# One of the two transfers that fill a key tile goes through GpSimd's queue instead of SyncE's

## The chip, the cores and the metric

The kernel runs on one core of a Trainium2 chip. A core has five engines that run their own instruction streams in order: TensorE (PE, matmuls), VectorE (DVE), ScalarE (ACT), GpSimd (POOL) and SyncE (SP, which here only issues transfers). They meet through semaphores. The metric is the device time of one execution in microseconds, taken as the median of three runs.

## The reference

The program computes a two-layer decoder trunk over 512 tokens of width 1024, with 16 heads of 64, in float32. Layer 0 has stick-breaking attention, layer 1 a dilated attention with rotary keys and queries; a gated feed-forward of width 2816 follows each.

```python
def _stick_breaking(q, k, v):          # per block of 128 queries
    z = jnp.einsum('bhqd,bhkd->bhqk', qb, kh).astype(jnp.float32) * scale
    log_stay = jnp.where(strict, jax.nn.log_sigmoid(-z), 0.0)
    log_after = lax.cumsum(log_stay, axis=3, reverse=True) - log_stay
    w = jnp.where(strict, jnp.exp(jax.nn.log_sigmoid(z) + log_after), 0.0)
    return jnp.einsum('bhqk,bhkd->bhqd', w, vh.astype(jnp.float32)).astype(q.dtype)
...
for layer in range(DEPTH):
    hn = _rmsnorm(h, norm_mix[layer])
    if layer < N_A_LAYERS:
        q, k, v = jnp.split(hn @ w_qkv_a[layer], 3, axis=-1)
        ...
        h = h + _stick_breaking(q, k, v).reshape(b, s, d) @ w_o_a[layer]
    else:
        kv = _rmsnorm(h, norm_kv) @ w_kv
        ...                             # rotary on the keys
        q = _rope((hn @ w_q_b[j]).reshape(b, s, N_HEADS, HEAD_DIM))
        h = h + _dilated_attention(q, kv_blocks).reshape(b, s, d) @ w_o_b[j]
    h = h + _swiglu(_rmsnorm(h, norm_ffn[layer]), w_gate[layer], w_up[layer], w_down[layer])
return _rmsnorm(h, norm_final)
```

## The kernel before

Every product is made of three matmuls on values split in a high and a low half (`mm3`, line 389): high by high, high by low, low by high. The activations lie transposed in the core's memory, channels on partitions and 512 tokens along the free axis. The stages are layer 0's attention, its feed-forward, layer 1's attention and its feed-forward.

In an attention layer the heads go in eight pairs p, heads 2p and 2p+1; this text numbers heads through both layers, 0 to 15 in layer 0 and 16 to 31 in layer 1. For each pair a projection makes 128 channels, two heads of 64, in one bank of PSUM. ACT, DVE and, in layer 1, the rotary step (`rope`, line 551, whose swap of half-heads is itself four transfers) bring it to a tile that `split_base` (line 519) splits: ACT writes the high half of a tile `hl` (line 522), DVE the low half (line 523). Then transfers rearrange it. `to_moving` (line 532) makes the key tile `mov` of each head: one head's 64 partitions of `hl`, high and low, are laid twice, into partitions 0 to 63 and 64 to 127. That is two transfers of 256 KB a tile, four a pair, 64 in all. `to_stationary` (line 539) does the like for the queries (`sta`). The scores of a head are seven matmuls z<-mov,sta (`scores`, line 639); `softmax` or `stick_breaking` makes weights of them, transposes (line 710) turn these, ACT and DVE split them into `ah` and `al` (lines 716 and 717), and `av` (line 723) multiplies with the values. Tile rings hold four `mov` tiles and two `hl`.

What fills TensorE beside a head's scores and values are pieces of the next pairs' projections. `attention` (line 733) writes the order of these pieces per head, and a scheduling layer, which has its own expectation of how long each instruction and transfer takes, sets the final fixed order of each engine's instructions. Each engine then runs in that order, and an instruction whose semaphore has not come stops everything behind it on the same engine.

SP's queue issues all transfers: the weights `raw` (line 243, 400 of them, each waiting for its ring place), `mov`, `sta`, the rotary swap `rp` (line 564), inputs and output. POOL does small things: zeros in `w`, `ah` and `al` (lines 663, 714, 715); in layer 1 the product of weights with a norm's gain (line 305) and the sine half of the rotary step (line 566); in the feed-forward a product (line 977).

Of the kernel before, what the change touches and what calls it, by code (L numbers as in the profile page):

```python
# [7 lines left out]
F = mybir.dt.float32  # L8
# [320 lines left out]
def trunk(ctx, tc, xg, wflat, cst_d, cs_d, outT):  # L329
    nc = tc.nc  # L330
    pe, act, dve, pool, sp = nc.tensor, nc.scalar, nc.vector, nc.gpsimd, nc.sync
# [26 lines left out]
    def T(name, dt=F, k=1):  # L358
        shape = [128, 512] if k == 1 else [128, k, 512]
        return rings["pool"].tile(shape, dt, name=name, bufs=rings["n"][name])  # L360
# [171 lines left out]
    def to_moving(p, hl):  # L532
        for i in range(2):
            t = T("mov", FR, 2)
            for j in range(2):
                sp.dma_start(t[64 * j:64 * j + 64].bitcast(F), hl[64 * i:64 * i + 64].bitcast(F))
            MOV[2 * p + i] = t

    def to_stationary(p, hl):
# [37 lines left out]
    def mov_pieces(layer, p):  # L577

        return proj_pieces(lambda b: to_moving(p, split_base(position(layer, b, p), 1.0)))
# [180 lines left out]
    def mixer(layer, slot0, gain_next):  # L760
        vslot = lambda p: (slot0 + p) % 9
        oslot = lambda p: (slot0 + 8 + p) % 9
        with phase(f"at{layer}", B_RINGS if layer else A_RINGS):
            def whole(fs_done):
                for f in fs_done[0]:
# [5 lines left out]
            both("qk", pair, dict(zip((3, 5, 7), rstd_steps(zb))) if layer else {})  # L771
            ends = [lambda: to_stationary(0, split_base(position(layer, pair[0], 0), 0.125)),
                    lambda: to_moving(0, split_base(position(layer, pair[1], 0), 1.0))]
            v_first, v_last = v_pieces(0, vslot, zb if layer else zbank)
            if layer == 0:
# [396 lines left out]
```

## Time and profile before

| | us |
|---|---|
| median of three runs | 1205.92 (1204.87 to 1207.19) |
| the profiled execution | 1206.22 |
| its span, first to last instruction | 1204.4 |
| TensorE busy in the span | 1185.6 (98%) |
| VectorE | 1014.0 (84%) |
| ScalarE | 698.2 (58%) |
| GpSimd | 178.6 (15%) |

The mean granted clock of TensorE is 0.997 of full. The profile's page and the trace are read so: times count from the span's first instruction, L536 is line 536 of the kernel, and tiles are named out<-in without their buffer numbers. SPq is SP's queue; a row of it shows the issue of transfers and not their movement. Idle time of an engine is put down to what ended it.

### The profile page before, as it was taken

How to read it: one execution, taken by the hardware profiler on the slowest of the kernel's cores; microseconds unless marked ns; L12 is line 12 of the kernel's file. 1: busy time of each engine (PE TensorE's matmuls, PEld its weight loads, DVE VectorE, ACT ScalarE, POOL GpSimd, SP SyncE). 2: the span in 40 equal slices, each digit the busy share in tenths (PEclk: the TensorE clock that was granted, in tenths of full speed). 3: DMA queues.
4: the chain of work that ended last, by engine and by line, in shares of the span. 5: the costliest groups of instructions: out<-in, count | busy, mean ns of one | idle time of the engine just before them, and what ended most of it. 6: DMA issues, size and time to landing. Idle time of an engine off the chain costs nothing.

```text
span 1204.4 us, 21111 instructions
## 1 busy us (share of the span) xinstructions
PE 1185.6 (98%) x7501; PEld 1059.6 (88%) x7501; DVE 1014.0 (84%) x1825; ACT 698.2 (58%) x1331; POOL 178.6 (15%) x245
## 2 busy tenths in 40 slices
PE   9999999999999999999999999999999999999997
PEld 7989888878999999999788888888889999999996
DVE  6799999899987878786868899788999978787865
ACT  6667676685545444454466677767755444445443
POOL 0000000011100000014234343110111000000111
PEclk9999999999999999999999999999999999999998
DMA  7654644234243334333154556551343333333122
GB/s 265 177 145 116 158 115 125 62 105 140 88 131 90 114 89 115 95 106 88 36 149 128 151 134 175 141 149 53 97 141 117 120 99 103 98 114 89 45 61 70
DMA packets 74361, 138.31 MB, mean 115 GB/s; under 512 B 9616, under 2 KB 13712, under 8 KB 74256
## 3 DMA queue, kind: packets, MB, share of 16 engines
q1 hardware_dynamic: 74256, 136.97, 40.0%
q8 instruction: 59, 0.97, 0.3%
q14 instruction: 46, 0.38, 0.1%
HBM read 106.00 MB, written 2.10 MB: 90 GB/s over the span
## 4 chain that ended last, share of the span: by engine, by line
PE 83%; issue 6%; DVE 5%; DMA 3%; POOL 1%; SPq 1%; ACT 1%; POOLq 0%; DVEq 0%; ACTq 0%
PE pj L387 38%; PE z L387 29%; PE t L387 10%; PE av L387 3%; PE t L710 3%; DMA raw<-wflat 1%; DVE wlo L307 1%; DMA mov<-hl 1%; DMA rp<-rp 1%; DVE H L758 1%; DVE sum L280 0%; DVE w2lo L307 0%; SPq L243 0%; DMA H<-xg 0%; POOL H L1085 0%
## 5 line engine op out<-in xcount | busy, mean ns | idle before, releaser
L306 ACT ACTIVATE whi<-raw 128x512 fp32r<-128x512 f32 (+1 forms) x290 | 178.4, 620 | 132.3 <-PE pj L387 51.2
L307 DVE TENSOR_TENSOR wlo<-raw,whi 128x512 fp32r<-128x512 f32 (+1 forms) x290 | 204.9, 714 | 25.4 <-ACT whi L306 23.1
L387 PE MATMUL pj<-VO,whi 128*128 128x512 f32 x568 | 180.8, 398 | 1.1 <-DVE H L758 1.0
L387 PE MATMUL pj<-X,whi 128*128 128x512 f32 x480 | 154.7, 402 | 0.3 <-ACT X L423 0.2
L977 POOL TENSOR_TENSOR up<-up,R 128x512 f32<-128x512 f32 x40 | 62.1, 1559 | 494.3 <-DVE up L1025 445.4
L387 PEld LDWEIGHTS pj<-VO,whi 128*128 128x128 f32 x568 | 102.4, 189 | 23.5 <-DVE H L758 2.1
L387 PE MATMUL pj<-VO,wlo 128*128 128x512 f32 x284 | 112.7, 397 | 0.0
L758 DVE TENSOR_TENSOR H<-H,pj 128x512 f32<-128x512 f32 (+1 forms) x120 | 79.2, 663 | 32.1 <-PE pj L387 31.4
L387 PEld LDWEIGHTS pj<-X,whi 128*128 128x128 f32 x480 | 87.0, 189 | 19.0 <-ACT X L423 1.0
L387 PE MATMUL z<-XT,whi 128*128 128x256 f32 x560 | 99.7, 280 | 0.0
L306 ACT ACTIVATE w2hi<-raw 128x512 fp32r<-128x512 f32 (+1 forms) x102 | 62.6, 616 | 58.0 <-PE z L387 16.6
L387 PE MATMUL z<-X,whi 128*128 128x256 f32 (+1 forms) x464 | 96.0, 301 | 0.0
L387 PE MATMUL pj<-X,wlo 128*128 128x512 f32 x240 | 95.2, 397 | 0.2 <-DVE wlo L307 0.2
L387 PEld LDWEIGHTS z<-XT,whi 128*128 128x128 f32 x560 | 86.2, 189 | 0.7
L387 PE MATMUL pj<-VO,w2hi 128*128 128x512 f32 x264 | 83.2, 396 | 0.6 <-ACT VO L983 0.4
L307 DVE TENSOR_TENSOR w2lo<-raw,w2hi 128x512 fp32r<-128x512 f32 (+1 forms) x102 | 69.8, 688 | 11.4 <-ACT w2hi L306 11.1
L387 PEld LDWEIGHTS z<-X,whi 128*128 128x128 f32 x464 | 74.9, 189 | 4.7
L387 PE MATMUL z<-XT,wlo 128*128 128x256 f32 x280 | 78.5, 280 | 0.0
L387 PE MATMUL pj<-whi,X 128*128 128x256 f32 x384 | 74.9, 284 | 2.1 <-DVE rp L565 2.1
L387 PE MATMUL z<-XT,w2hi 128*128 128x256 f32 x400 | 73.6, 283 | 0.1
L305 POOL TENSOR_TENSOR raw<-raw,H 128x512 f32<-128x512 f32 x48 | 57.5, 1209 | 82.5 <-DMA raw<-wflat 55.5
L387 PE MATMUL z<-X,wlo 128*128 128x256 f32 (+1 forms) x232 | 69.8, 301 | 0.0
(204 smaller groups left out, 3042.6 us busy)
## 6 DMA issues: line engine op xcount, KB each, us to landing
raw<-wflat SPq DMA_DIRECT2D x384, 256.0 KB, 2.8
mov<-hl SPq DMA_DIRECT2D x64, 256.0 KB, 4.4
sta<-hl SPq DMA_DIRECT2D x64, 128.0 KB, 2.3
rp<-rp SPq DMA_DIRECT2D x56, 64.0 KB, 2.2
raw<-wflat SPq DMA_DIRECT2D x16, 128.0 KB, 2.2
H<-xg SPq DMA_DIRECT2D x7, 256.0 KB, 5.3
outT<-H SPq DMA_DIRECT2D x2, 512.0 KB, 3.1
CS<-cs SPq DMA_DIRECT2D x1, 512.0 KB, 3.7
```

Of the source, the lines that this page charges most:

```text
L305: nc.gpsimd.tensor_mul(v3, v3, g.unsqueeze(2).to_broadcast([128, n // m, m]))
L306: nc.scalar.activation(hi[:, :n], v, AF.Copy)
L307: nc.vector.tensor_sub(lo[:, :n], v, hi[:, :n].bitcast(F))
L387: pe.matmul(out, a, b, start=start, stop=stop, skip_group_check=True)
L710: pe.transpose(b[:, o:o + 128], pr[i][:, 128 * c:128 * c + 128], idf)
L758: dve.tensor_add(H[:, n, e], H[:, n, e], p[:, e])
L977: pool.tensor_mul(two(u), two(u), r)
```

## The change

In `to_moving` the second transfer of each key tile, the one into partitions 64 to 127, is issued from POOL's queue. SP keeps the first.

```diff
             for j in range(2):
-                sp.dma_start(t[64 * j:64 * j + 64].bitcast(F), hl[64 * i:64 * i + 64].bitcast(F))
+
+                (sp, pool)[j].dma_start(t[64 * j:64 * j + 64].bitcast(F), hl[64 * i:64 * i + 64].bitcast(F))
```

Lines behind it have a number one higher in the changed kernel. The scheduling layer answers with other orders on all engines. On TensorE, at head 18 (tile mov_7441, first of layer 1's second pair), this stood in a row before, z_7675, z_7703 and z_7719 being the head's scores, t the transposes of an earlier head's weights and pj_7654 a projection:

```order
L710 MATMUL t_7685<-cst_67,z_7511 128x128
L710 MATMUL t_7685<-cst_67,z_7483 128x128
L710 MATMUL t_7695<-cst_67,z_7553 128x128
L710 MATMUL t_7695<-cst_67,z_7511 128x128
L710 MATMUL t_7695<-cst_67,z_7483 128x128
L387 MATMUL pj_7654<-X_62,whi_7518 128x512 x2
L387 MATMUL pj_7654<-X_62,wlo_7519 128x512
L387 MATMUL pj_7654<-X_62,whi_7518 128x512 x2
L387 MATMUL pj_7654<-X_62,wlo_7519 128x512
L387 MATMUL z_7675<-mov_7441,sta_7347 128x512 x2
L387 MATMUL z_7703<-mov_7441,sta_7347 128x384 x2
L387 MATMUL z_7719<-mov_7441,sta_7347 128x256 x3
```

and this stands there now:

```order
L711 MATMUL t_7685<-cst_67,z_7511 128x128
L387 MATMUL z_7675<-mov_7441,sta_7347 128x512 x2
L711 MATMUL t_7685<-cst_67,z_7483 128x128
L711 MATMUL t_7695<-cst_67,z_7553 128x128
L711 MATMUL t_7695<-cst_67,z_7511 128x128
L711 MATMUL t_7695<-cst_67,z_7483 128x128
L387 MATMUL z_7703<-mov_7441,sta_7347 128x384 x2
L387 MATMUL pj_7654<-X_62,whi_7518 128x512 x2
L387 MATMUL pj_7654<-X_62,wlo_7519 128x512
L387 MATMUL pj_7654<-X_62,whi_7518 128x512 x2
L387 MATMUL pj_7654<-X_62,wlo_7519 128x512
L387 MATMUL z_7719<-mov_7441,sta_7347 128x256 x3
```

The first scores stand ahead of four transposes and six projection matmuls that were ahead of them.

On TensorE at head 20 (tile mov_7887, first of the third pair), the difference between the two orders has this piece, in which the scores z_8008, z_8036 and z_8085 are added:

```order
 L387 MATMUL pj_8100<-wlo_7929,X_62 128x256
 L387 MATMUL pj_8100<-whi_7928,X_62 128x256 x2
+L387 MATMUL z_8008<-mov_7887,sta_7767 128x512 x2
+L387 MATMUL z_8036<-mov_7887,sta_7767 128x384 x2
+L387 MATMUL z_8085<-mov_7887,sta_7767 128x256 x3
 L387 MATMUL pj_8100<-wlo_7929,X_62 128x256
 L387 MATMUL pj_8100<-whi_7928,X_62 128x256
```

Before, they stood 30 matmuls later, behind the rest of this projection's piece, four transposes and most of head 19's product with the values; they have been moved past all of it.

On VectorE, ahead of the same head's keys, this stood in a row before: hl_7884 is the low half that the transfers of heads 20 and 21 wait for, wlo a split weight, ACC an addition behind an earlier head, rp the rotary step:

```order
L307 TENSOR_TENSOR wlo_7983<-raw_7569,whi_7982 128x512
L565 TENSOR_TENSOR rp_7963<-pj_7893,CS_66 128x512
L567 TENSOR_TENSOR rp_7875<-rp_7875,rp_7874 128x512
L307 TENSOR_TENSOR wlo_8047<-raw_7602,whi_8046 128x512
L630 TENSOR_TENSOR ACC_65<-av_7941,tf_8005 64x512
L523 TENSOR_TENSOR hl_7884<-rp_7875,hl_7884 128x512
```

and this now:

```order
L566 TENSOR_TENSOR rp_7963<-pj_7893,CS_66 128x512
L568 TENSOR_TENSOR rp_7875<-rp_7875,rp_7874 128x512
L307 TENSOR_TENSOR wlo_7983<-raw_7569,whi_7982 128x512
L523 TENSOR_TENSOR hl_7884<-rp_7875,hl_7884 128x512
L307 TENSOR_TENSOR wlo_8047<-raw_7602,whi_8046 128x512
L631 TENSOR_TENSOR ACC_65<-av_7941,tf_8005 64x512
```

One weight split and the addition went from before hl_7884 to behind it.

Head 24 has its scores moved forward on TensorE in the same way, past part of a projection, and head 22 past two transposes; in layer 0 only head 0's first scores move, past six projection matmuls.

## Rows read from the trace of the kernel before

**Rows 1.** Windows of the attention layers: length, busy us of PE, PEld, DVE, ACT, POOL

```profile
30.00:232.00 202.00, 202.00 (x1165) 175.57 (x1164) 179.21 (x320) 135.90 (x280) 9.97 (x78) 1.00 0.50 131
586.00:834.00 248.00, 243.07 (x1379) 209.14 (x1378) 204.49 (x501) 167.25 (x377) 73.94 (x87) 1.00 0.50 131
```

**Rows 2.** TensorE's waits in layer 1's attention: total us, times, longest us

```profile
PE pj L387 <- DVE rp L565: 2.1, 1, 2.1
PE z L387 <- DMA mov<-hl: 1.5, 3, 0.7
PE av L387 <- DVE al L717: 1.3, 3, 0.7
```

**Rows 3.** Timeline around head 18's scores: start us, us, engine, line, operation, out<-in, [idle]

```profile
649.26 3.18 SPq L536 DMA_DIRECT2D mov<-hl  x4
...
651.36 0.82 PE L710 MATMUL t<-cst,z 128*128 128x128 f32 x6
...
653.84 0.88 PE L387 MATMUL z<-mov,sta 128*128 128x512 f32 x3 [0.26 <-DMA mov<-hl]
```

**Rows 4.** The key tile's own view: its transfers, from issue to landing

```profile
DMA to landing us min/median/max: 2.9/4.4/5.6
```

**Rows 5.** Chain that ended last, at head 18's keys: start us, us, what

```profile
649.81 3.90 DMA mov<-hl
```

**Rows 6.** Groups of instructions on POOL, the gain product: count, busy us, mean ns

```profile
L305 POOL TENSOR_TENSOR raw<-raw,H 128x512 f32<-128x512 f32 x48 | 57.5, 1209 | 82.5 <-DMA raw<-wflat 55.5 <-DVE s L1015 13.7 <-DVE st L688 6.8
```

**Rows 7.** Timeline around head 0's scores

```profile
32.32 3.23 SPq L536 DMA_DIRECT2D mov<-hl  x4
...
36.66 0.63 PE L387 MATMUL pj<-X,whi 128*128 128x512 f32 x2
...
38.06 0.63 PE L387 MATMUL z<-mov,sta 128*128 128x512 f32 x2
```

**Rows 8.** Timeline around head 4's scores

```profile
77.63 3.65 SPq L536 DMA_DIRECT2D mov<-hl  x4
...
82.87 0.71 PE L387 MATMUL z<-mov,sta 128*128 128x512 f32 x2
```

**Rows 9.** Timeline around head 20's keys and scores

```profile
677.14 2.49 POOL L305 TENSOR_TENSOR raw<-raw,H 128x512 f32<-128x512 f32 x2
...
677.21 1.51 DVE L567 TENSOR_TENSOR rp<-rp 128x512 f32<-128x512 f32 x1 [0.59 <-POOL rp L566]
...
678.65 1.52 DVE L307 TENSOR_TENSOR wlo<-raw,whi 128x512 fp32r<-128x512 f32 x1
...
678.76 0.63 ACT L522 ACTIVATE hl<-rp 128x512 fp32r<-128x512 f32 x1 [0.74 <-DVE rp L567]
...
680.70 1.18 DVE L523 TENSOR_TENSOR hl<-rp,hl 128x512 fp32r<-128x512 f32 x1
...
681.15 0.28 PE L387 MATMUL pj<-wlo,X 128*128 128x256 f32 x1
...
682.40 0.39 PE L387 MATMUL av<-al,VO 128*128 128x256 f32 x1 [0.72 <-DVE al L717]
...
683.33 0.68 DVE L567 TENSOR_TENSOR rp<-rp 128x512 f32<-128x512 f32 x1
...
686.52 0.70 PE L387 MATMUL z<-mov,sta 128*128 128x512 f32 x2 [0.54 <-DMA mov<-hl]
```

**Rows 10.** Timeline around the scores of heads 22 and 24

```profile
706.43 0.70 PE L387 MATMUL z<-mov,sta 128*128 128x512 f32 x2 [0.69 <-DMA mov<-hl]
...
732.81 0.36 PE L387 MATMUL pj<-whi,X 128*128 128x256 f32 x1
...
734.50 0.70 PE L387 MATMUL z<-mov,sta 128*128 128x512 f32 x2
```

**Rows 11.** Chain that ended last, at layer 1's first rotary keys

```profile
628.28 4.80 DMA rp<-rp
```

**Rows 12.** DMA issues of the page, the rotary swap: KB each, median us to landing

```profile
rp<-rp SPq DMA_DIRECT2D x56, 64.0 KB, 2.2
```

## Prediction

> **What bounds the kernel now.** I read the stages first, then who waits for whom, then the key tiles' own path. By stage [rows 1], TensorE is busy in 202.00 of the 202.00 us of layer 0's attention and in 243.07 of 248.00 us in layer 1's, so time can be won or lost only where the matmul queue stands still: about 5 us in layer 1, nothing in layer 0. The waits of layer 1 name what stops it [rows 2]: once the rotary output (2.1 us), three times the key transfers themselves (1.5 us), three times the low half of the attention weights (1.3 us). Key transfers are therefore on the path in layer 1, and just hidden in layer 0.
>
> One pair of heads costs four transfers, all on SP's queue: the row at 649.26 [rows 3] has four in 3.18 us. They land 2.9 us after issue at best, 4.4 in the middle and 5.6 at worst [rows 4]. For the tile of head 18 the second half was issued at 649.81, 0.55 after the first, and took 3.90 us to 653.71 [rows 5]; so an even tile is whole 4.45 us after its first issue. Its scores began at 653.84 after 0.26 us of idle [rows 3]: 0.13 us pass between landing and matmul.
>
> **The change part by part.** Removed: 32 of 64 issues on SP, about 1.6 us of each pair's 3.18 [rows 3]. Added: 32 transfers on POOL's queue, each pair behind a wait for the low half of `hl` by DVE. Nothing in the trace shows a transfer issued by POOL, so I bound the shift of an even tile, s, from both sides. Below: both halves land as the quickest does, 2.9 us after the wait, against 4.45, so s = -1.5. Above: POOL needs as long for one issue as for its gain product, 1.21 us [rows 6], and the transfer then takes the worst landing: 1.21 + 5.6 - 4.45 = +2.4. I take s = 1.21 - 0.55 = +0.66, rounded to +0.6: POOL starts 1.21 us late, but the half no longer stands 0.55 us behind its sister. Odd tiles gain, but nobody is waiting for them.
>
> The Trainium skill bears on the low bound. Its page "DMA: Bandwidth & Descriptors", section "Rules for kernel authors", says that spreading transfers over issuing engines brings no bandwidth, because the same 16 engines carry them; it saves issue time alone. By that rule s could not be -1.5, about 0 at best; the sum below does not use it, and no run here shows it yet.
>
> The scheduler also answers to the edit: it expects keys earlier and puts their scores ahead of other work in TensorE's fixed order. A matmul placed too early stops everything behind it. Term by term:
>
> - Head 0: the first half was issued at 32.32, so the tile is whole near 36.77 (an estimate, + 4.45), and its scores stand at 38.06 [rows 7]. They now stand six projection matmuls earlier, at 36.66. With s they can start at 36.77 + 0.6 + 0.13 = 37.50: cost 0.8 us.
> - Heads 4, 8, 12 (their place is kept): 77.63 + 4.45 + 0.6 + 0.13 = 82.81 against the score's 82.87 [rows 8]: cost 0. The cover is TensorE's earlier work; it is thin, so each 0.1 us that s is above 0.66 costs 0.1 three times.
> - Head 18: the scores move to behind the second of six transposes, that is 651.57 in the old times (651.36 plus two steps, an estimate from 0.82 us for six that overlap [rows 3]). The keys come at 653.84 at the old pace, with s at 654.44. The idle is 2.87 instead of 0.26: cost 2.6 us. The work it was moved past comes afterwards and no longer hides the transfer.
> - Head 20: all seven score matmuls move from 686.52 to just before 681.15 [rows 9]. DVE's order moves too: `hl` goes ahead of a weight split begun at 678.65 and an addition, and could start when ACT's half is done (678.76 + 0.63 = 679.4) instead of 680.70 [rows 9], 1.3 us sooner. The scores then start at 686.52 - 1.3 + 0.6 = 685.8. The work jumped over lasts 686.52 - 681.15 = 5.37 us less its two idles (0.72 and 0.54), 4.1 us, and follows the scores. TensorE reaches the old end 685.8 + 4.1 - 686.5 = 3.4 us late. This is a total, not on top of head 18's 2.6, if the keys don't slide with TensorE; it is on top if they do.
> - Head 22 jumps two transposes in front of a wait of 0.69 us [rows 10]: 0.2 + s, about 0.8.
> - Head 24 moves from 734.50 to 732.81 [rows 10], where there is no idle now: 1.7 + s = 2.3.
>
> If no lateness carries over, layer 1 costs 3.4; if all does, 2.6 + 3.4 + 0.8 + 2.3 = 9.1. The keys come out of TensorE's own projections, but through ACT, DVE, POOL and transfers with waits of their own; I take a third of the way, 5.3. Against it stands SP's relief. The rotary transfer of 4.80 us [rows 11] had queued behind four key and four weight transfers; its kind takes 2.2 in the middle [rows 12], and TensorE lost 2.1 us to that chain [rows 2]. The new order also fills that gap with other projections, but head 18's keys then arrive no sooner, which is why I credit only 1.5. Sum: 0.8 + 5.3 - 1.5 = +4.6 us. What is queued behind POOL's new waits (memsets in layer 0, gain and rotary products in layer 1) costs nothing in the sum, since no wait in [rows 2] names POOL as the one that came last; if a gain product came late by the two issues' 2.4 us, the weights would be used up at once and that would appear as a new wait.
>
> The profiled execution took 1206.22 us (span 1204.4); 1206.2 + 4.6 = 1210.8. It ran 0.3 above the median shown, so for a median I say 1210.5.
>
> **The rivals.**
>
> 1. *No change*: no lateness carries over, and the work that the scores were moved past fills all the other idle of layer 1. For it: the three kinds of waits in [rows 2] sum to only 4.9 us and can swap places; against it: layer 0 has no idle to give. Sum: 0.8 + 3.4, less 2.1 (rotary), 1.3 (attention weights) and 0.7 (head 22), is +0.1: time 1206.3.
> 2. *Faster*: two queues work side by side, halves land together, s = -1.5. Every s above becomes 2.1 smaller: head 0 costs nothing, head 18 costs 0.5, and the total at head 20 is 3.4 - 2.1 = 1.3, the only lateness if none carries over. Off that go the rotary wait (2.1), the waits for attention weights (1.3), which displaced work now fills, and head 22's 0.69 [rows 2, 10]: 1.3 - 2.1 - 1.3 - 0.7 = -2.8, time 1203.4. It decides from s below about -1.3, and only if nothing carries over. Against it: the four scores moved forward use up whatever the tile gains.
> 3. *Much slower*: POOL can't issue while DVE works. For it: the two engines slow each other in the trace; the same DVE rotary addition takes 1.51 us at 677.21, while POOL is at work from 677.14, and 0.68 at 683.33 when it is alone [rows 9]. If each issue waits out two such DVE instructions, 3 us, s is about +2.4. Heads 4, 8 and 12 then cost 1.75 each (5.2), head 0 2.6, layer 1 about 5.3 + 4 x 1.8 = 12.5 before the credit of 1.5. Sum +19, time 1225; with half of it absorbed, 1216. Against it: POOL's row there is a product that reads two operands, and an issue reads none. The Trainium skill has the mechanism on its page "SBUF — State Buffer", section "SBUF: two separate sides": GpSimd writes the descriptors of its own transfers and is locked out while DVE runs in a two-port mode. The trace agrees only in that the pair slows down together.
>
> **How the numbers follow.** Forecast 0.55, no change 0.21, faster 0.12, much slower 0.12. 0.2% of this kernel is 2.4 us, about what a measurement tells from no change. Of the forecast's own spread (1207.5 to 1215) a little falls within that, of rival 1 a little beyond: faster 0.12, same 0.23, slower 0.65. The range 1203.5 to 1219 leaves out half of the faster case and the upper half of the much slower one.
>
> **What would show it.** In the profile after: POOL has 32 transfers, SP 32 fewer; the second half of an even tile lands 4.5 to 5.5 us after DVE's `hl`; TensorE waits for keys four to six times in layer 1, 1 to 3 us each at heads 18, 20 and 24, against 1.5 us in all now; the 2.1 us wait for rotary output is gone or shorter; layer 0 grows by about 1 us at its first head and nowhere else; both feed-forward stages keep their length. I am wrong if the waits for keys sum to less than 3 us (the scheduler's guess was good), if layer 0 grows by over 3 us (POOL's issue is far dearer than 1.21 us), or if the time is lost in new waits for weights.

## The result and the profile after

The changed kernel takes 1221.72 us (median of four, 1217.85 to 1224.95) beside 1206.2 for the kernel before on the same chip: a ratio of 1.0130, 95% interval 1.0116 to 1.0144, or 15.5 us more. The prediction had the side right and the size wrong: 4.6 us more was forecast (1210.5), and 1221.7 lies above its range.

The profiled execution after took 1224.95 us (span 1223.1); it is the slowest of the four, 3.2 above their median. Windows of the two attention layers, with the columns of [rows 1] (length, busy us of PE, PEld, DVE, ACT, POOL, granted clock, DMA share, GB/s), and under them four stretches of layer 1:

```profile
30.00:235.00 205.00, 202.13 (x1160) 175.12 (x1159) 178.92 (x320) 135.51 (x279) 18.11 (x94) 1.00 0.50 129
589.00:852.00 263.00, 249.66 (x1378) 215.43 (x1377) 204.97 (x501) 168.88 (x376) 79.76 (x103) 0.97 0.48 124
658.50:661.80 3.30, 3.30 (x12) 2.91 (x11) 2.42 (x8) 1.80 (x4) 0.02 (x1) 0.50 0.84 240
692.60:695.90 3.30, 3.30 (x17) 3.28 (x15) 3.04 (x11) 0.00 (x0) 0.94 (x1) 0.50 0.98 255
743.80:750.50 6.70, 5.75 (x24) 5.56 (x25) 4.75 (x10) 1.18 (x3) 3.12 (x3) 0.50 0.61 163
801.80:805.20 3.40, 3.40 (x9) 2.62 (x9) 3.40 (x13) 2.06 (x4) 0.00 (x0) 0.50 0.66 151
```

Layer 0 grew by 3 us, layer 1 by 15, and what lies between kept its length. New is the third number from the right: in four stretches of layer 1, 17 us together, TensorE ran at half of its clock, 1.2 GHz. The profile of before has the half level only from 1196.8 us on, at the last matmuls. TensorE's waits, first layer 1's (which answers to [rows 2]), then layer 0's, where the same view of the kernel before is empty:

```profile
PE z L387 <- DMA mov<-hl: 8.3, 3, 3.3
PE pj L387 <- DVE rp L566: 2.3, 1, 2.3
PE z L387 <- issue: 1.2, 1, 1.2
PE t L711 <- DVE z L697: 1.0, 1, 1.0
PE av L387 <- DVE al L718: 0.5, 1, 0.5
```

```profile
PE z L387 <- issue: 2.5, 1, 2.5
PE pj L387 <- DVE tq L549: 0.4, 1, 0.4
```

Waits for keys in layer 1 rose from 1.5 us to 9.5 (8.3 by name, and 1.2 put down to "issue" at head 16, whose keys landed 0.1 us before its scores). The other three are at heads 18, 20 and 24. From the timeline the scores of head 16, head 18's surroundings, which answer to [rows 3], and the scores of heads 20 [rows 9] and 24; the columns are start, length, engine, line, operation, tiles and idle before:

```profile
630.22 1.05 PE L387 MATMUL z<-mov,sta 128*128 128x512 f32 x4 [1.25 <-issue]
...
653.43 1.14 SPq L537 DMA_DIRECT2D mov<-hl  x2
...
653.65 1.08 POOL L537 DMA_DIRECT2D mov<-hl  x2 [0.84 <-DVE hl L523]
...
654.82 0.38 PE L711 MATMUL t<-cst,z 128*128 128x128 f32 x2
...
657.79 0.73 PE L387 MATMUL z<-mov,sta 128*128 128x512 f32 x2 [2.58 <-DMA mov<-hl]
...
658.36 0.97 PE L711 MATMUL t<-cst,z 128*128 128x128 f32 x4
...
692.03 2.07 PE L387 MATMUL z<-mov,sta 128*128 128x512 f32 x7 [3.34 <-DMA mov<-hl]
...
744.75 1.86 PE L387 MATMUL z<-mov,sta 128*128 128x512 f32 x4 [2.33 <-DMA mov<-hl]
```

Head 18's scores stand behind the second transpose, the four others follow them, and TensorE stands for 2.58 us where it stood for 0.26. The seven scores of head 20 take 2.07 us, most of it at half clock; before, the chain that ended last has them in 1.41:

```profile
686.52 1.41 PE z L387 x7
```

The transfers themselves, with the issue's duration (min, median, max ns), the landing (min, median, max us, which answers to [rows 4]), and the median by queue:

```profile
L537 POOL DMA_DIRECT2D mov<-hl x32: 509/512/720, 31.1 to 812.9; - x32
L537 SPq DMA_DIRECT2D mov<-hl x32: 462/538/762, 32.0 to 812.6; - x32
...
DMA to landing us min/median/max: 3.0/5.2/8.0
```

```profile
mov<-hl POOLq DMA_DIRECT2D x32, 256.0 KB, 5.7
mov<-hl SPq DMA_DIRECT2D x32, 256.0 KB, 5.1
```

POOL issues as fast as SP, 0.51 us, right behind DVE's low half; yet the transfers land later on both queues than the 4.4 of before.

### The profile page after: what moved, and what is told of

Same layout as the page of the kernel before. It is cut to its first block, busy times and chain, and to the rows that moved or that the text cites. A ratio compares the mean times of both kernels' runs of the same rounds, so it can differ in the third digit from the quotient of the medians.

```text
span 1223.1 us, 21168 instructions
## 1 busy us (share of the span) xinstructions
PE 1193.3 (98%) x7501; PEld 1066.3 (87%) x7501; DVE 1015.6 (83%) x1825; ACT 699.8 (57%) x1331; POOL 192.3 (16%) x277
## 4 chain that ended last, share of the span: by engine, by line
PE 81%; DVE 6%; issue 6%; DMA 3%; ACT 1%; POOL 1%; SPq 0%; POOLq 0%; DVEq 0%; ACTq 0%
PE pj L387 36%; PE z L387 29%; PE t L387 10%; PE av L387 3%; PE t L711 2%; DVE wlo L307 1%; DMA mov<-hl 1%; DMA raw<-wflat 1%; DVE H L759 1%; DMA rp<-rp 1%; DVE sum L280 0%; DVE rp L568 0%; DVE w2lo L307 0%; DVE z L689 0%; DVE sum L281 0%
## 5 line engine op out<-in xcount | busy, mean ns | idle before, releaser
L307 DVE TENSOR_TENSOR wlo<-raw,whi 128x512 fp32r<-128x512 f32 (+1 forms) x290 | 207.9, 724 | 28.0 <-ACT whi L306 25.7
```

What stands on the lines that cost most here:

```text
L307: nc.vector.tensor_sub(lo[:, :n], v, hi[:, :n].bitcast(F))
```

## The experiments

The change does two things at once: it moves transfers, and it makes the scheduling layer write another order. The first two runs take these apart. A function pins every engine to a list of instructions; it adds no waits, only an order of issue (the last run of this section, pinned too, takes as long as the kernel before, so the pinning costs nothing that can be seen):

```diff
+def hold(nc, tc):
+    traced = {i.name: i for i in nc.cur_bb.bb.instructions}
...
+            if prev is not None:
+                tc.add_manual_dep(i, prev.name, mybir.DependencyInfo(
+                    mybir.DependencyClass.NoSync, mybir.DependencyReason.DATA), reason="hold")
+            prev = i
...
         trunk(ctx, tc, *ins, out)
+        hold(nc, tc)
```

**The queue without the order.** The changed kernel, with the list of the kernel before on every engine:

> The second halves go out from POOL as in the change, but every engine keeps the order of issue of the kernel before (POOL's 32 transfers stand where SP issued their first halves). Theory A, the new order of the matmuls is what costs: an even tile is whole 4.3 to 4.75 us after its first issue in the changed kernel's trace against 4.45 before, so the old order stalls about as before, plus near 1.2 us at head 0, whose SP half took 6.8 us: 1205 to 1209 us. Theory B, the transfers themselves are slower on two queues (halves of up to 8.0 us against 5.6) and would stall any order: 1215 us or more. Theory A also expects the granted clock at full through layer 1 and waits for keys of under 3 us in all.

Measured: 1209.9 us (1209.08 to 1215.19) against 1205.8, ratio 1.0045 (1.0025 to 1.0066), about 5 us. Theory B falls as the main cause. Theory A is nearly met in time and not in the rest: the profiled execution, 1215.19 us and the slowest of the five, waits 6.0 us for keys in layer 1 and another 1.3 at head 16 that is put down to "issue", more than twice what was allowed, and the clock fell twice. POOL's part in the waits, at head 20 (the timeline):

```profile
682.48 0.92 DVE L525 TENSOR_TENSOR hl<-rp,hl 128x512 fp32r<-128x512 f32 x1
...
682.82 1.75 POOL L568 TENSOR_TENSOR rp<-rp,CS 128x512 f32<-128x512 f32 x1
683.43 1.14 SPq L538 DMA_DIRECT2D mov<-hl  x2
...
684.53 1.49 POOL L307 TENSOR_TENSOR raw<-raw,H 128x512 f32<-128x512 f32 x1
685.96 1.08 POOL L538 DMA_DIRECT2D mov<-hl  x2
...
689.93 1.43 PE L389 MATMUL z<-mov,sta 128*128 128x512 f32 x5 [2.23 <-DMA mov<-hl]
```

SP issues when `hl` is there; POOL is in two products of its own and comes 2.5 us later. In the changed kernel's own order POOL's transfers come right behind `hl`, so this part belongs to the mix of the new queue with the old order.

**The order without the queue.** The kernel before, all transfers on SP, with the changed kernel's list:

> All 64 transfers stay on SP, each second half right behind its first, but every engine has the order of issue of the changed kernel. Theory A, the order costs: the scores of heads 18, 20 and 24 stand before their keys as in the changed kernel, whose waits there were 2.6, 3.3 and 2.3 us, and the clock falls behind them: 1213 to 1220 us. Theory B, the second queue costs: the old queue brings the keys in time, 1205 to 1209 us. Under both, head 0 loses less than its 2.5 us, since its SP half no longer lands 6.8 us after issue.

Measured: 1217.06 us (1215.04 to 1220.13), ratio 1.0095 (1.0076 to 1.0113), about 11 us, as theory A had it. So the order alone costs about 11 us and the queue alone about 5; together 17, equal to the 15.5 of the whole within the intervals.

**The moved scores alone.** All transfers on SP and the order of before, but the scores of heads 0, 18, 20, 22 and 24 at their new places in TensorE's list. (In the changed order head 21's scores stand 13 matmuls earlier as well, and head 29's 12 later; those two stay where they were.) At head 20 the list reads

```diff
 L389 MATMUL pj_8100<-whi_7928,X_62 128x256 x2
+L389 MATMUL z_8008<-mov_7887,sta_7767 128x512 x2
+L389 MATMUL z_8036<-mov_7887,sta_7767 128x384 x2
+L389 MATMUL z_8085<-mov_7887,sta_7767 128x256 x3
 L389 MATMUL pj_8100<-wlo_7929,X_62 128x256
...
```

> All transfers on SP and the order of the kernel before, except that the score matmuls of heads 0, 18, 20, 22 and 24 stand where the changed kernel has them. Theory S, those scores make the loss that the order makes: by the prediction's terms without their share for the queue 0.2 + 2.0 + 2.8 + 0.2 + 1.7 = 6.9 us if all carries over, and up to 1.7 us for each half-clock stretch, 1212 to 1218 us (the whole order cost 11.2). Theory R, the rest of the order (projections, attention outputs, the orders of DVE and ACT) makes most of it: under 1210 us.

Measured: 1217.4 us (1213.8 to 1219.75), ratio 1.0084 (1.0064 to 1.0104): as much as the whole order. Theory S holds; the reordered projections and DVE's order are worth nothing that can be seen, which here means less than about 3 us. Its waits in layer 1 (total us, times, longest):

```profile
PE z L389 <- DMA mov<-hl: 8.7, 3, 5.2
PE z L389 <- issue: 2.0, 1, 2.0
PE pj L389 <- DVE rp L567: 1.1, 1, 1.1
PE av L389 <- DVE al L719: 0.8, 1, 0.8
```

The same run shows how lateness travels. First issue of each pair's keys, against the kernel before:

| pair of head | before | moved scores | later by |
|---|---|---|---|
| 18 | 649.26 | 648.95 | -0.31 |
| 20 | 681.90 | 684.97 | 3.07 |
| 22 | 701.75 | 711.02 | 9.27 |
| 24 | 729.88 | 739.83 | 9.95 |
| 28 | 775.66 | 789.21 | 13.55 |

TensorE itself is 3.10 us late at the 4100th matmul (664.52 before), between heads 18 and 20, and 9.24 at the 4300th (697.86), ahead of head 22. The next keys slide with it, whole. In the changed kernel, whose order has other projections moved too, the keys of heads 20, 22, 24 and 28 are issued 5.34, 5.12, 10.10 and 13.97 us late, 2.84 of that already there at head 16: by the end of the layer the same slide, with a stop at head 22.

**The clock, with the moved scores.** Matmuls whose results are overwritten fill most of the three waits; `h` counts within the layer, so that 2, 4 and 8 are heads 18, 20 and 24:

```diff
+FILL = {2: 7, 4: 19, 8: 6}
...
         b = zb()
+        if u == 0 and scores.layer == 1:
+            for _ in range(FILL.get(h, 0)):
+                mm(b, q[:, 0:128], q[:, 0:512], True, True)
```

> The run with the moved scores alone, plus 7, 19 and 6 matmuls of 512 columns, whose results are overwritten, directly in front of the first scores of heads 18, 20 and 24: 1.6, 4.4 and 1.4 us of work in waits of 2.1, 5.2 and 2.0. Theory C, the clock is the second part of the order's price: the three stretches at half clock behind these waits (3.41, 6.83 and 3.41 us, worth up to 6.8) go, and what stays is the growth of the waits themselves, 1.9 + 3.9 + 0.7 + 2.0 = 8.5 us at heads 18, 20, 22 and 24: 1211 to 1214.5 us. Rival, the clock gives nothing back, because DVE and the transfers set the pace behind a wait: 1217 us.

Measured: 1215.35 us (1214.78 to 1215.78), ratio 1.0086 (1.0071 to 1.0102): above theory C, below its rival. The half clock is gone, as the granted clock (third from the right) of the same window without and with the filling shows:

```profile
685.00:696.00 11.00, 6.43 (x30) 6.26 (x31) 3.17 (x6) 1.12 (x2) 1.25 (x3) 0.69 0.42 95
```

```profile
685.00:696.00 11.00, 9.81 (x65) 8.82 (x64) 5.14 (x16) 2.28 (x4) 0.81 (x3) 1.00 0.56 128
```

Only 2 us of the median came back, and by the ratios, 1.0084 and 1.0086, nothing. Either most of what half-clock matmuls lose would have been idle a little later anyway, or the filling costs something itself; no run tells these apart. The spread of the four executions fell from 6 us to 1.

**The clock, in the changed kernel.** The same with its own order and 8, 11 and 7 matmuls:

> The changed kernel with its own order held, and 8, 11 and 7 matmuls of 512 columns, whose results are overwritten, put directly in front of the first scores of heads 18, 20 and 24; at 0.234 us each they fill 1.9, 2.6 and 1.6 us of the 2.6, 3.3 and 2.3 us in which TensorE stood there. Theory A, part of the loss is the granted clock, which read 0.5 for 3.41, 3.41 and 6.83 us behind these three waits: those stretches go, up to half of their 13.65 us, 4 to 7 us come back, 1214.5 to 1218 us, with one stretch at half left near 800 us. Rival, the clock is a by-product and the time is set by DVE, ACT and the transfers: 1221 to 1223 us.

Measured: 1218.72 us (1217.93 to 1219.36), ratio 1.0106 (1.0091 to 1.0121): 3.0 us of the median back, just short of what theory A asked; the intervals of the two ratios just touch. No stretch at half was left in layer 1, not even near 800 us; one appeared behind head 0's wait.

The four executions of the changed kernel had mean granted clocks of 0.995, 0.993, 0.994 and 0.990 and spans of 1216.0, 1219.6, 1220.1 and 1223.1 us: how often the clock falls differs between executions, and the profiled one had the most of it. Over the 74 executions of the changed kernel and of the experiments, each beside the mean of its own kernel, the span grows by about 1.1 us for each 0.001 that the clock is lower (an estimate). As 0.001 of such a span is 2.4 us at half clock, 1.2 us would be the price with none of it hidden. That speaks for a half clock that costs nearly its full price, but does not show it: a longer wait can lengthen the execution and bring the clock down at once.

**Layer 0 alone, and without its first pair.**

```diff
+                q = pool if j and layer == 0 else sp
+                q.dma_start(t[64 * j:64 * j + 64].bitcast(F), hl[64 * i:64 * i + 64].bitcast(F))
```

> Only layer 0's second halves go out from POOL, layer 1's stay on SP; the order is made anew. If each layer's loss stands for itself, layer 0 keeps its 3.1 us (2.4 of them at head 0) and layer 1 has its old rows: 1208 to 1210 us. Rival, the loss in layer 1 starts from layer 0's lateness or from its order: 1214 us or more. A second rival, head 0's loss is taken up by a later wait as in the kernel before: 1206 us.

The second run has this line instead:

```diff
-                q = pool if j and layer == 0 else sp
+                q = pool if j and layer == 0 and p else sp
```

> As the run with layer 0 alone, but the first pair of layer 0 (heads 0 and 1) keeps SP for all four transfers; TensorE's order is then that of the kernel before. If layer 0's loss is head 0 alone (a wait of 2.2 us there, and the half-clock stretch behind it), 1205 to 1207 us. Rival, the other even heads also cost, each tile being whole 0.5 to 0.9 us later than before and their cover being 0.5 to 0.7 us: 1208 us or more.

Measured: 1209.89 us (1208.53 to 1213.59), ratio 1.0035 (1.0020 to 1.0051), and without the first pair 1205.45 (1204.3 to 1209.44), ratio 0.9994 (0.9982 to 1.0007). Layer 0's loss is head 0 and, within the 2 us that the second ratio's interval leaves, nothing else, though the even tiles there land later: at head 4 of the second run it is whole 5.45 us after its first issue (4.76 before), and the scores follow 0.05 us behind the landing. The cover named in the prediction was just enough. Layer 1's waits in the first run have before's form again, so its loss does not start in layer 0.

**Layer 1 alone.** The same edit with `layer == 1`:

> Only layer 1's second halves go out from POOL; the order is made anew and is that of the changed kernel but for head 0. If the losses of the layers add up, this is the changed kernel less what layer 0 alone cost (1.0130 less 0.0035): 1.0095, about 1217 us, with waits for keys of 2 us and more at heads 18, 20 and 24. Rival, an unhurried layer 0 leaves layer 1 the time to hide part: 1213 us or less.

Measured: 1219.85 us (1217.73 to 1223.34), ratio 1.0112 (1.0077 to 1.0147), with waits for keys of 3.07, 3.25 and 2.35 us at heads 18, 20 and 24. The layers add up, 1.0035 and 1.0112 against 1.0130, within the intervals; nothing is hidden by a faster layer 0.

**Which half is served first.** Two runs with before's order held. In one SP issues only the first of a pair's four transfers:

```diff
-                (sp, pool)[j].dma_start(t[64 * j:64 * j + 64].bitcast(F), hl[64 * i:64 * i + 64].bitcast(F))
+                (sp, pool)[i or j].dma_start(t[64 * j:64 * j + 64].bitcast(F), hl[64 * i:64 * i + 64].bitcast(F))
```

> The order of the kernel before is held; SP issues only the first half of an even tile, POOL the other three. Theory O, overtaking: four halves of a pair share the same 16 engines and land about 1.2 us apart (652.23, 653.71, 654.92, 656.07 at head 18 before), and with both second halves on POOL the odd tile's first half passes the even tile's second (654.01, 655.29, 656.49, 658.07, the third of which completes the even tile). Here nothing can pass it: the even tile is whole 4.0 to 4.6 us after its first issue instead of 5.64, and the time is 1205 to 1208 us. Theory P, a transfer issued by POOL is slow by itself: the tile is whole 5.4 us or more after its first issue, the time 1209 to 1211 us.

In the other SP issues the even tile and POOL the odd one:

```diff
-                (sp, pool)[j].dma_start(t[64 * j:64 * j + 64].bitcast(F), hl[64 * i:64 * i + 64].bitcast(F))
+                (sp, pool)[i].dma_start(t[64 * j:64 * j + 64].bitcast(F), hl[64 * i:64 * i + 64].bitcast(F))
```

> The order of the kernel before is held; SP issues both halves of the even tile, POOL both of the odd one. Theory O: the even tile's second half stands behind its sister on SP and meets at most one half of the odd tile: whole 4.45 to 5.1 us after its first issue, the odd tile 1 us later than before, 1205 to 1208 us. Theory P: the even tile at 4.45 as before, 1206 us, and only the odd tile is late, where head 21 has 0.4 us to spare and would wait near 1 us.

Measured: 1208.85 us, ratio 1.0028 (1.0018 to 1.0037), with three on POOL; 1212.07, ratio 1.0052 (1.0037 to 1.0067), with the odd tile on POOL. Landing of the four halves after the pair's first issue, from the transfers' completions in the traces (e1, e2 the halves of the even tile, o1, o2 of the odd one, P where POOL issued; "second halves" is the run of the queue without the order):

```
before,        head 18:  e1 2.98   e2 4.45   o1 5.66   o2 6.81
second halves, head 18:  e1 3.16   o1 4.44   e2 5.64P  o2 7.22P
three on POOL, head 18:  e1 3.10   e2 5.13P  o1 7.01P  o2 8.62P
odd on POOL,   head 4:   e1 4.47   o1 4.73P  e2 6.78   o2 6.97P
before,        head 4:   e1 3.44   e2 4.76   o1 6.04   o2 7.07
```

Overtaking is there: with one queue the four come 1.0 to 1.5 us apart in the order of issue; with two, a half of the odd tile passes the even tile's second and pushes it back 1.2 us (second line) or 2 us (fourth). It depends on when POOL issues. With the odd tile on POOL, POOL came 0.8 us behind SP at heads 18, 20 and 24, and there the even tile was whole after 4.49 to 4.55 us, as on one queue; at the others it came at most 0.5 us behind (0.27 at head 4), the even tile was late, and TensorE waited 1.0 to 2.4 us at heads 4, 16, 22 and 28. In the changed kernel's own order POOL issues the even tile's half ahead of SP's next one at heads 18, 20 and 24, and it is not overtaken there.

Where nothing can pass, three on POOL, the even tile of head 18 gains 0.5 us but stays 0.7 behind one queue, for POOL's half took 4.36 us from its own issue where SP's second took 3.90 [rows 5] behind a sister. That does not make a transfer from POOL slow by itself, as theory P has it: at head 20 of the same run POOL issued when SP's half had all but landed, and its half took 2.87 us, as long as SP's quickest (2.9, [rows 4]), from the chain that ended last:

```profile
683.87 2.87 DMA mov<-hl
```

So theory O is right on the mechanism and too cheap. At head 18 SP, with three key transfers less to issue, sent a weight transfer at 651.12, 1.0 us behind POOL's half, where the kernel before sends it behind all four; whether that makes the 0.5 us no run shows. Neither division beats one queue.

**Even and odd tile, order made anew.** The edit of the last run without the list:

> The same division as in the run before, SP the even tile and POOL the odd one, but the order is made anew. If the scheduler again puts scores ahead, because it expects their keys sooner from two queues: waits for keys of 2 us and more in layer 1, half-clock stretches behind them, 1212 us or more. If it expects the even tile as late as with one queue, the order stays near the old one and the time is 1205 to 1209 us.

Measured: 1218.47 us (1213.93 to 1223.15), ratio 1.0103 (1.0072 to 1.0134), with waits of 2.5 and 2.6 us at heads 18 and 20 and two stretches at half clock behind them. The scheduler moved scores forward here too, but less: head 20's by 11 matmuls (30 in the changed kernel), head 18's by one (10). At both heads the even tile was overtaken and whole only after 5.61 and 5.73 us (4.45 and 4.48 before), which is about half of each wait.

**The other way round.** All transfers on SP, before's list, and TensorE's scores a little later. At heads 18 and 20 the list reads

```diff
+L389 MATMUL pj_7654<-X_62,whi_7564 128x512 x2
+L389 MATMUL pj_7654<-X_62,wlo_7565 128x512
 L389 MATMUL z_7675<-mov_7441,sta_7347 128x512 x2
...
+L389 MATMUL av_8121<-ah_8131,VO_63 128x512
+L389 MATMUL av_8121<-al_8132,VO_63 128x512
 L389 MATMUL z_8008<-mov_7887,sta_7767 128x512 x2
...
```

> The opposite of what the changed order does: all transfers on SP, every engine in the order of the kernel before, but TensorE gets head 18's scores behind three projection matmuls more, head 20's behind two attention outputs, an attention output before that behind six small projections, and three projections ahead of the outputs and scores of head 22. If what counts is only that nothing stands in front of its keys, the waits of 0.26, 0.72, 0.54, 0.22 and 0.69 us of the kernel before shrink by 1.5 to 2.1 us in all: 1203.4 to 1204.5 us. Rival, the waits move on to the next instruction that depends on them (DVE's chain sets them): 1205.5 us.

Measured: 1205.61 us against 1205.23, ratio 0.9998 (0.9987 to 1.0009): the rival. The waits changed place [rows 2]:

```profile
PE pj L389 <- DVE rp L567: 1.9, 1, 1.9
PE z L389 <- DMA mov<-hl: 1.5, 2, 0.8
PE av L389 <- DVE al L719: 1.1, 1, 1.1
PE z L389 <- issue: 0.5, 1, 0.5
```

Head 18's is gone, those of heads 20 and 22 are no shorter than before, 0.78 and 0.73 (0.54 and 0.69), and head 24 has one of 0.53: more work in front of the scores did not take the waits away. No version beat the kernel before.

## Why the prediction was right in kind and wrong in size

The mechanism was right: scores were put ahead of their keys and TensorE stood. What failed is what was said to follow from such a wait.

*The carry-over, the step that failed most.* Its words were "I take a third of the way, 5.3", between 3.4 (nothing carries over) and 9.1 (all does). Nearly all does: in the run with the moved scores the next pairs' keys were issued 3.07, 9.27 and 13.55 us late, as late as TensorE was. The reason given against it, that keys pass through ACT, DVE, POOL and transfers "with waits of their own", did not hold: that chain begins at a matmul, and its waits took up nothing of the lateness in those rows. Waits for keys in layer 1 grew by 8.0 us (1.5 to 9.5). Of the single terms head 18 was close (it stood 2.58 us, 2.87 forecast) and head 24 too (2.33, 2.3 forecast); head 22, put at 0.8, did not stand at all, and head 16, at nothing, stood 1.25. The last two misses partly cancel, which is luck.

*Head 20.* Its term of 3.4 us counted on DVE making `hl` 1.3 us sooner. The lists ahead show that while one weight split went behind `hl`, another (wlo_7983) came to stand between the rotary step and `hl`:

```profile
683.62 0.69 DVE L568 TENSOR_TENSOR rp<-rp 128x512 f32<-128x512 f32 x1 [0.58 <-POOL rp L567]
...
684.23 1.53 DVE L307 TENSOR_TENSOR wlo<-raw,whi 128x512 fp32r<-128x512 f32 x1
...
685.68 1.52 DVE L523 TENSOR_TENSOR hl<-rp,hl 128x512 fp32r<-128x512 f32 x1
```

From the end of the rotary step to the first key transfer 2.93 us pass (684.31 to 687.24), and 3.18 before (678.72 to 681.90): 0.25 us were gained, not 1.3. TensorE stood there 3.34 us.

*The clock, which no term had.* Behind waits of 2.3 to 3.3 us TensorE ran at 1.2 GHz for 3.4 or 6.8 us. In the profiled execution that is 17 us at half, at most 8.5 lost, and in the three others less; filling the three waits at heads 18, 20 and 24 gave back 3.0 of the median, and at the same places without the second queue 2 us, which is not clear of noise.

*Head 0.* Forecast 0.8, found a wait of 2.49 us and a layer 0 that is 3 us longer (alone 4.2, 2.4 to 6.1). The even tile was taken as whole 4.45 us after its first issue, plus s:

```profile
30.19 1.75 SPq L544 DMA_DIRECT2D sta<-hl  x3
...
31.07 1.24 POOL L537 DMA_DIRECT2D mov<-hl  x2 [26.39 <-DVE hl L523]
...
32.03 1.38 SPq L537 DMA_DIRECT2D mov<-hl  x2
...
39.02 0.70 PE L387 MATMUL z<-mov,sta 128*128 128x512 f32 x2 [2.49 <-issue]
```

POOL does not stand behind SP's query transfers and issues both its halves 0.96 us ahead of SP's first. They landed at 35.34 and later; SP's half, issued at 32.03, landed at 38.82, 6.8 us on. That the queue which was relieved would become the slow one was not considered. It takes both parts of the change: head 0 waited 0.24 us with the new order alone and 0.52 with the queue alone.

*s.* Forecast +0.6, from an issue of 1.21 us. The issue is 0.51 us. In layer 1 s came out at -0.1 to +0.3 at heads 18, 20 and 24 (whole after 4.31, 4.75 and 4.73 against 4.45 to 4.52), but at +1.1 at head 22, where nobody waited, and at +2.5 at head 16 (6.86 against 4.36), which is the wait that no term had; in layer 0 it was +0.1 at head 2 and +0.5 to +0.9 from head 4 on. The mean of the 15 pairs behind head 0 is 0.6: the right size by luck, for what the cheap issue saved, sharing took back. Odd tiles, said to gain, did not: head 19's was whole 7.80 us after the pair's first issue, against 6.81. The Trainium skill, "DMA: Bandwidth & Descriptors", section "Queues, rings and completion order", says that each DMA engine takes the queues in turn, a packet at a time; the traces agree, with halves of two queues that were issued 0.27 us apart and took 4.46 us each (e1 and o1 of the fourth line above), where the first half took 3.44 on one queue. The rule of the Trainium skill that the prediction cites, from which it took s as "about 0 at best", is borne out too: in no run with two queues was an even tile that TensorE waited for whole more than 0.14 us sooner than before.

*Heads 4, 8 and 12 at nothing.* Right, and as thin as stated (0.05 us at head 4).

*The credit of 1.5 for SP's relief.* Not paid. The rotary wait went from 638 to 801 us and stayed 2.3; with a new wait for DVE (1.0) and the smaller one for attention weights (0.5) these come to 3.8, against 3.4.

Put together for the profiled execution: head 0 and layer 0 3, keys 8.0, other waits 0.4, clock up to 8.5: up to 20, against 18.7 of span. At the median, against 4.6 forecast: 3.8 for the carry-over, 1.5 for the credit, 2 to 3 for layer 0, 3 for the clock, 14.9 to 15.9, and 15.5 measured. This is an account made afterwards and not a test: layer 0's and the clock's parts are each known to about 2 us only. The rival "much slower" had the time, 1216 to 1225, by a mechanism that is not there: POOL's issues take 0.51 us while DVE works beside them.

What stays open: what made POOL's half 0.5 us slower than SP's at head 18 with nothing passing it, why head 16's second half took so long, how much the half clock costs, and how the queue's 5 us in the old order, part of which is POOL's late issue at head 20, divides in the new one.

## What to carry to other kernels

A moved transfer can change less by itself than through the order that a scheduler rebuilds on its guess of it: compare the orders first, and price each instruction that was moved in front of its data at the full wait. On an engine that is 98% busy expect lateness to be handed on whole, as here, unless a row shows idle time downstream that is there for another cause. The second queue did not bring a pair's four transfers in sooner (the last after 7.22 us against 6.81 at head 18) and gave up their order of service; no division of the queues that was tried made this kernel faster.

## What the runs showed of the hardware

- A transfer issued by POOL costs POOL 0.51 us, as much as SP (0.54), and it waits its turn behind POOL's products (2.5 us at head 20 of the queue's own run).
- The clock's fall does not follow from a wait's length alone: half clock came behind 1.86 us (the run with later scores: granted clock 0.50 from 638.3 to 641.6), 2.24 us (head 0 with layer 0 alone) and 2.58 us (head 18 after), and not behind 2.08 us (before, at 638 [rows 2]) and 2.49 us (head 0 after).
- On one queue the four transfers of a pair, 256 KB each, land 1.0 to 1.5 us apart (heads 4 and 18 above); on two queues two of them can land 0.3 us apart, and the last of the four comes at about the same time (6.97 us against 7.07 at head 4, 7.22 against 6.81 at head 18). Their 4 KB packets take 304 ns (median) before and 311 on POOL's queue after, so 64 packets on 16 engines are 1.2 us (an estimate from these): the spacing on one queue is that of the engines, and not that of the issues, 0.55 us for the first two.
- A transfer from POOL is not slow by itself: 2.87 us at head 20 with three halves on POOL, when SP's half had all but landed, against 2.9 for SP's quickest before [rows 4].
